# Inverse roots of a hybrid layer: the logarithm reads the sum of squares itself, and the correction takes three vector steps

## The chip, the cores and the metric

The kernel runs on one core of a Trainium2 chip. The metric is the device time in microseconds of one execution: the median of the runs shown. A core has engines that run side by side, each its own instructions in order: TensorE for matrix products (PE in the profile, its weight loads PEld), VectorE (DVE), ScalarE (ACT), GpSimd (POOL) and SyncE (SP), which here only issues transfers. Matrix products write to PSUM, a small memory of banks; everything else stands in SBUF. Instructions wait for each other through semaphores.

## What is computed

One layer over 576 frames: 512 of a new stream (the prompt) and 64 of a running one (the sample), 2048 channels each. All of it is float32.

```python
def rmsnorm(x, g):
    y = xf * lax.rsqrt(jnp.mean(xf * xf, axis=-1, keepdims=True) + EPS) * g

hn = rmsnorm(x, g_norm1)
q, k, v, gb, gc, hc = split(hn @ w_in)
q = rmsnorm(q.reshape(B, T, N_HEADS, HEAD_DIM), g_q)      # 8 heads of 128
k = rmsnorm(k.reshape(B, T, N_HEADS, HEAD_DIM), g_k)
o_attn = stick_breaking_blocks(q, k_all, v_all, P)
u = gc * hc
o_conv = gb * conv3(u)
mix = concat([rmsnorm(o_attn, g_attn_out), rmsnorm(o_conv, g_conv_out)])
x = x + mix @ w_out
h2 = rmsnorm(x, g_norm2)
x = x + (silu(h2 @ w_gate) * (h2 @ w_up)) @ w_down
```

There are six norms, each with an inverse root 1/sqrt(sum/n + EPS), EPS = 1e-6. The one of `g_norm1` is made with a power on GpSimd and is not touched. The other five go through the function that the change edits.

## The kernel before

**Layout.** Channels lie on the 128 partitions and frames along the free dimension, in two halves of 288 frames (`HALF`, `HALVES`). Nearly every vector or scalar instruction on activations is therefore 128x288. Each float32 operand of a product is split into a high and a low part (`split`, L221: a ScalarE copy rounds to the high part, a VectorE subtraction leaves the low part), and a product takes three matrix products (high by high, low by high, high by low; `step`, L210). Weights come by transfer and are split in the same way, 1024 columns at a time (`weight_parts`, L174, and later L1005 and L1008, L222 and L223).

**Stages.** Heads: for each of eight heads the products for q, k and v (`head`, `project`, `product`), and between them, in small pieces, the attention of the head before. Then the convolution channels (`conv_group`, `conv_run`), the output projection (`out_proj`), the gate and up products and the down products of the feed-forward part (`run`). The products after the second convolution group run by a scheme with seven products in place of eight, whose operands are sums and differences of blocks; `head_forms` makes those of the attention's output.

**Order.** TensorE's order is written out by hand. An object `pipe` counts products: after each three, `pipe.tick` lets generators that are due issue their next piece; `yield 13` means thirteen ticks later. VectorE's and ScalarE's orders are chosen by the framework's scheduler from the dependencies when the kernel is built, except in a few stretches under `manual_schedule`, where the program's order holds: the start up to L441, the stretch from the second convolution group (L934) to L1181, and the end from L1782.

**The inverse root.** `rsqrt_mean(dst, src, n, width)` (L456) gets in `src` the sum of squares over the channels, already on all partitions. `channel_sums` (L468) makes it with two matrix products by a matrix of ones, into a PSUM bank of the pair `misc`. The function then runs

- L461, VectorE: `ms = src / n + EPS`, out of PSUM into SBUF;
- L462 and L463, ScalarE: `y = exp(-0.5 ln(ms))`, a first value of the inverse root;
- L464, L465, L466, VectorE: one Newton correction, `dst = (1.5 - 0.5 ms y y) y`.

It is called from five places, for two halves each: `norm_evac` for q and for k of each head (L628; 32 calls), `head_forms` for the attention's output (L537; 2), `group_scale` for the convolution's output (L576; 2), `row_scale2` for the second norm (L1775; 2). In `norm_evac` the result `r` scales q or k (L629), which is then split for the attention scores (L679).

**The pair of banks `misc`.** `misc` (L260) hands out two PSUM banks in turn. A tile of it can be written only when the readers of the tile two before it are done. Its users in the heads are the sums (`ss`), the sample's scores (`zs`, L705), the weighted values (`po`, L744; `os`, L777) and the sample's cumulated logarithms (`cz`, L763). In a head past the first two the order on TensorE is: sums of q (two halves), `po`, sums of k first half, `cz`, sums of k second half, `os`, `zs`. So the tile two after the sums of k first half is that of the sums of k second half. In the first head the four sums stand in a row, two ticks or so apart (`lags`).

Of the kernel before, what the change touches and what calls it, by code (L numbers as in the profile page):

```python
# [10 lines left out]
F32 = mybir.dt.float32  # L11
F32R = mybir.dt.float32r
AF = mybir.ActivationFunctionType
ALU = mybir.AluOpType
PSUM = bass.MemoryType.PSUM

P = 128
# [3 lines left out]
HALF = T // 2  # L21
# [10 lines left out]
EPS = 1e-6  # L32
# [62 lines left out]
def tile_hybrid_stream_step(  # L95
# [6 lines left out]
    nc = tc.nc  # L102
# [13 lines left out]
    rpool = ctx.enter_context(tc.tile_pool(name="rpool", bufs=1, side="left"))  # L116
    tmp = ctx.enter_context(tc.tile_pool(name="tmp", bufs=2, side="left"))
# [44 lines left out]
    def weight_raw(i):  # L162
        src, nk, ncol = specs[i]
        raw = raw_tile["A"][:, i % 2, : nk * ncol]
        return raw, raw.rearrange("p (k c) -> p k c", k=nk), src
# [55 lines left out]
    def split(hi, lo, src, lo_eng=None):  # L221
        nc.scalar.copy(out=hi, in_=src)  # L222
        (lo_eng or nc.vector).tensor_tensor(out=lo, in0=src, in1=hi.bitcast(F32), op=ALU.subtract)  # L223
# [149 lines left out]
    with tc.manual_schedule(engines={mybir.EngineType.Activation, mybir.EngineType.DVE, mybir.EngineType.SP}):  # L373
        raw, raw3, src = weight_raw(0)
# [25 lines left out]
        for kt in range(KD + LAG):  # L400
# [21 lines left out]
            if kt == 16:  # L422
                nc.vector.tensor_tensor(out=lo1[:, :1024], in0=raws[1][:, :1024], in1=hi1[:, :1024].bitcast(F32),  # L423
                                        op=ALU.subtract)
# [28 lines left out]

    hpool.release()

    def rsqrt_mean(dst, src, n, width, ms=None, t=None):  # L456
        if ms is None:
            ms = tmp.tile([P, HALF], F32, tag="ms", name="ms", bufs=1)[:, :width]
            t = tmp.tile([P, HALF], F32, tag="t", name="t", bufs=1)[:, :width]
        y = tmp.tile([P, HALF], F32, tag="y", name="y")[:, :width]  # L460
        nc.vector.tensor_scalar(out=ms, in0=src, scalar1=1.0 / n, scalar2=EPS, op0=ALU.mult, op1=ALU.add)  # L461
        nc.scalar.activation(out=y, in_=ms, func=AF.Ln)  # L462
        nc.scalar.activation(out=y, in_=y, func=AF.Exp, scale=-0.5)  # L463
        nc.vector.tensor_tensor(out=t, in0=y, in1=y, op=ALU.mult)  # L464
        nc.vector.scalar_tensor_tensor(out=t, in0=t, scalar=-0.5, in1=ms, op0=ALU.mult, op1=ALU.mult)  # L465
        nc.vector.scalar_tensor_tensor(out=dst, in0=t, scalar=1.5, in1=y, op0=ALU.add, op1=ALU.mult)  # L466

    def channel_sums(src_hi, src_lo, a, b, name):  # L468
        ps = misc(name)[:, : b - a]
        mm(ps, oner, src_hi, start=True, stop=False)  # L470
        mm(ps, oner, src_lo, start=False, stop=True)
        return ps
# [10 lines left out]
    for i in range(5):  # L483
        n = P if i < 4 else TS
        nc.vector.tensor_scalar(out=dg[:n, i, :n], in0=ident[:n, :n], scalar1=rst[:n, i : i + 1], scalar2=None,
                                op0=ALU.mult)
# [40 lines left out]
    def head_forms():  # L527
# [8 lines left out]
        for (sh, sl), (a, b) in zip(two, HALVES):  # L536
            rsqrt_mean(acc_a[:, a:b], channel_sums(sh, sl, a, b, "ssg"), 8 * P, HALF)  # L537
            yield 4
# [28 lines left out]
    def group_scale(acc, dst, rows_of):  # L567

        four = cpool.tile([P, 2, 2, HALF], F32R, tag="uc", name="sqg")
        for i, (a, b) in enumerate(HALVES):  # L570
            sh, sl = four[:, i, 0], four[:, i, 1]
            split(sh, sl, acc[:, a:b])
            yield rows_of
            ss = channel_sums(sh, sl, a, b, "ssg")
            ms, t = (tmp.tile([P, HALF], F32, tag=tag, name=tag + "g") for tag in ("r", "sq"))
            rsqrt_mean(dst[:, a:b], ss, 8 * P, HALF, ms, t)  # L576
            yield rows_of

    acc_a = rpool.tile([P, T], F32, tag="R", name="acc_a", bufs=2)
# [39 lines left out]
    def norm_evac(name, gcol, dst_f, dst_hi, dst_lo, first, after=None):  # L619
        E = t1.tile([P, T], F32, tag="E", name=f"E{name}", bufs=2)  # L620

        def rest(a, b, sh, sl):
            if first:
                lags[0] += 4
            yield 6 + lags[0] if first else 16 if after else 13
            ss = channel_sums(sh, sl, a, b, "ss")
            r = tmp.tile([P, HALF], F32, tag="r", name="r")
            rsqrt_mean(r, ss, P, HALF)  # L628
            nc.vector.scalar_tensor_tensor(out=dst_f[:, a:b], in0=E[:, a:b], scalar=gcol, in1=r,  # L629
                                           op0=ALU.mult, op1=ALU.mult)  # L630
            e = min(b, TP)
            split(dst_hi[:, a:e], dst_lo[:, a:e], dst_f[:, a:e])
            if after and b == T:
                pipe.spawn(after)

        def evac(ps, a, b):
            nc.vector.tensor_tensor(out=E[:, a:b], in0=ps, in1=R1[:, a:b], op=ALU.mult)
            sq = tmp.tile([P, HALF], F32, tag="sq", name="sq")
            sh, sl = parts("sq")
            nc.scalar.activation(out=sq, in_=E[:, a:b], func=AF.Square)  # L640
            split(sh, sl, sq)
            pipe.spawn(rest(a, b, sh, sl))

        return evac
# [467 lines left out]
    def open_out():  # L1112

        xpool.release()
        bt["y"] = ypool = tc.alloc_tile_pool(name="ypool", bufs=1, reuse_waits="tile", side="right")
        x2t.extend(ypool.tile([P, 2, T], F32, tag=f"y{j}", name=f"x2_{j}") for j in range(NP))
        bt["m"] = tc.alloc_tile_pool(name="mpool", bufs=1, reuse_waits="tile", side="right")
        bt["mc"] = [bt["m"].tile([P, n, 2, HALF], F32R, tag=tag, name=f"mix{tag}")
                    for n, tag in ((NG, "m0"), (NG - 1, "m1"), (1, "m1z"))]
        bt["R"] = rpool.tile([P, T], F32, tag="R", name="R_c", bufs=2)  # L1120
        pipe.spawn(load_rest())
        pipe.spawn(state_out())
        pipe.spawn(group_scale(bt["acc"], bt["R"], 7), 7 * 28)
# [53 lines left out]
    for k_, (n, p_) in enumerate(corder):  # L1177
# [7 lines left out]
        if n == NCU - 1 and p_ in (6, 7, 4):  # L1185
            q = {6: 1, 7: 2, 4: 3}[p_]
            t = bt["pool"].tile([P, NH, 2, HALF], F32R, tag=f"t{q}", name=f"forms{q}")
# [430 lines left out]
    for d, v in visits.items():  # L1618
        n = next(a for a, b in zip(v, v[1:]) if a >= NGU + 10 and b >= a + 4)
# [228 lines left out]
```

## Time and profile before

| | |
|---|---|
| median of 3 runs | 2372.15 us (2371.21 to 2373.49) |
| the profiled execution, its own time | 2373.26 us |
| its span, first to last instruction | 2371.6 us |
| mean granted TensorE clock | 0.999 |
| TensorE busy | 2348.9 us, 99% of the span |
| VectorE, ScalarE, GpSimd busy | 81%, 49%, 12% |

Rows of groups of instructions give line, engine, operation, output and inputs, shape, count, and times. Rows of a time line give start and duration in microseconds and then the same; a bracket at the end says how long the engine stood idle before the instruction and what it waited for. Rows of waits give who waited for whom, the total in microseconds, the number of waits and the longest.

### The profile page before, as it was taken

How to read it: one execution, taken by the hardware profiler on the slowest of the kernel's cores; microseconds unless marked ns; L12 is line 12 of the kernel's file. 1: busy time of each engine (PE TensorE's matmuls, PEld its weight loads, DVE VectorE, ACT ScalarE, POOL GpSimd, SP SyncE). 2: the span in 40 equal slices, each digit the busy share in tenths (PEclk: the TensorE clock that was granted, in tenths of full speed). 3: DMA queues.
4: the chain of work that ended last, by engine and by line, in shares of the span. 5: the costliest groups of instructions: out<-in, count | busy, mean ns of one | idle time of the engine just before them, and what ended most of it. 6: DMA issues, size and time to landing. Idle time of an engine off the chain costs nothing.

```text
span 2371.6 us, 44043 instructions
## 1 busy us (share of the span) xinstructions
PE 2348.9 (99%) x17653; PEld 2338.0 (99%) x17653; DVE 1927.6 (81%) x2892; ACT 1166.2 (49%) x2083; POOL 290.5 (12%) x386
## 2 busy tenths in 40 slices
PE   8999999999999999999999999999999999999999
PEld 8999999999999999999999999999999999999999
DVE  7868776788887889888888888888888778887876
ACT  6656655444444555444444444444444444444444
POOL 2111111332111230000000000000000002431211
PEclk9999999999999999999999999999999999999999
DMA  8465554683368654444444444444444936886642
GB/s 259 127 179 165 138 148 111 219 263 118 109 235 220 195 166 147 140 152 135 138 152 136 138 152 137 137 152 137 137 152 132 359 112 213 224 225 199 205 131 82
DMA packets 563845, 395.75 MB, mean 167 GB/s; under 512 B 67006, under 2 KB 552760, under 8 KB 563640
## 3 DMA queue, kind: packets, MB, share of 16 engines
q1 hardware_dynamic: 554296, 376.39, 50.6%
q0 software_dynamic: 8624, 16.22, 3.4%
q8 instruction: 138, 2.26, 0.4%
q14 instruction: 67, 0.55, 0.1%
q10 hardware_dynamic: 720, 0.33, 0.0%
HBM read 301.45 MB, written 91.44 MB: 166 GB/s over the span
## 4 chain that ended last, share of the span: by engine, by line
PE 90%; DVE 5%; DMA 2%; ACT 2%; issue 1%; POOL 0%; ACTq 0%; SPq 0%; DVEq 0%; POOLq 0%
PE psy L1532 34%; PE psw L1532 17%; PE pj L213 12%; PE psx L1532 8%; PE psy L1036 6%; PE pjo L213 4%; PE psw L1036 3%; PE psx L1036 2%; DMA raw_a<-in_w_down_dram 1%; DVE whl L223 1%; PE po L747 1%; PE z L679 1%; DVE whl L1008 0%; PE os L777 0%; DMA raw_a<-in_w_in_dram 0%
## 5 line engine op out<-in xcount | busy, mean ns | idle before, releaser
L1532 PE MATMUL psy<-h_s,whl 128*128 128x288 f32 x2787 | 413.5, 295 | 0.3 <-ACT part L1542 0.3
L213 PE MATMUL pj<-x,whi 128*128 128x288 f32 x1856 | 389.9, 297 | 0.3 <-DVE x L356 0.2
L1532 PEld LDWEIGHTS psy<-h_s,whl 128*128 128x128 f32 x2787 | 384.8, 189 | 0.6 <-ACT part L1542 0.5
L223 DVE TENSOR_TENSOR whl<-raw_a,whl 128x1024 fp32r<-128x1024 f32 (+4 forms) x296 | 321.1, 1086 | 61.3 <-ACT whl L222 60.4
L1532 PE MATMUL psw<-t,whl 128*128 128x288 f32 x2400 | 348.3, 295 | 0.0
L1532 PEld LDWEIGHTS psw<-t,whl 128*128 128x128 f32 x2400 | 327.5, 188 | 0.0
L222 ACT CAST whl<-raw_a 128x1024 fp32r<-128x1024 f32 (+4 forms) x296 | 267.8, 906 | 115.2 <-issue 35.4
L213 PEld LDWEIGHTS pj<-x,whi 128*128 128x128 f32 x1856 | 304.1, 189 | 1.5 <-DVE x L356 1.0
L213 PE MATMUL pj<-x,wlo 128*128 128x288 f32 x928 | 274.1, 295 | 0.1
L223 DVE TENSOR_TENSOR whl<-raw_b,whl 128x1024 fp32r<-128x1024 f32 (+5 forms) x190 | 201.6, 1061 | 69.2 <-ACT whl L222 68.1
L222 ACT CAST whl<-raw_b 128x1024 fp32r<-128x1024 f32 (+5 forms) x190 | 165.1, 871 | 167.8 <-issue 73.4
L1542 ACT COPY part<-psy 128x288 f32<-128x288 f32 x242 | 96.6, 399 | 281.4 <-PE psy L1532 279.6
L1532 PE MATMUL psy<-b22m,whl 128*128 128x288 f32 x1212 | 183.3, 295 | 0.2 <-ACT part L1542 0.2
L1532 PE MATMUL psy<-t2t,whl 128*128 128x288 f32 x1212 | 182.9, 294 | 0.0
L213 PEld LDWEIGHTS pj<-x,wlo 128*128 128x128 f32 x928 | 174.5, 188 | 0.7 <-DVE wlo L423 0.3
L1532 PE MATMUL psx<-h_s,whl 128*128 128x288 f32 x1185 | 173.6, 294 | 0.0
L1532 PEld LDWEIGHTS psy<-b22m,whl 128*128 128x128 f32 x1212 | 168.2, 188 | 0.4 <-ACT part L1542 0.4
L1532 PEld LDWEIGHTS psy<-t2t,whl 128*128 128x128 f32 x1212 | 167.9, 188 | 0.0
L1532 PEld LDWEIGHTS psx<-h_s,whl 128*128 128x128 f32 x1185 | 162.3, 188 | 0.0
L222 ACT CAST whl<-s 128x1024 fp32r<-128x1024 f32 (+5 forms) x81 | 72.2, 892 | 102.2 <-PE psw L1532 100.9
L1311 POOL DMA_DIRECT2D hid_dram<-form x3 | 2.3, 751 | 947.6 <-DVE form L223 947.6
L1532 PE MATMUL psy<-t,whl 128*128 128x288 f32 x576 | 107.7, 297 | 0.0
(471 smaller groups left out, 4408.7 us busy)
## 6 DMA issues: line engine op xcount, KB each, us to landing
hid_dram<-form SPq DMA_DIRECT2D x147, 288.0 KB, 2.3
raw_a<-in_w_in_dram SPq DMA_DIRECT2D x41, 1024.0 KB, 5.8
raw_a<-in_w_gate_dram SPq DMA_DIRECT2D x22, 1024.0 KB, 6.0
raw_a<-in_w_up_dram SPq DMA_DIRECT2D x22, 1024.0 KB, 5.7
raw_b<-in_w_gate_dram SPq DMA_DIRECT2D x22, 1024.0 KB, 6.7
raw_b<-in_w_up_dram SPq DMA_DIRECT2D x22, 1024.0 KB, 7.0
h_s<-hid_dram SPq DMA_DIRECT2D x10, 2016.0 KB, 12.5
raw_a<-in_w_out_dram SPq DMA_DIRECT2D x16, 1024.0 KB, 5.6
```

Of the source, the lines that this page charges most:

```text
L213: mm(ps, w_[:, k, csl], x_, start=(k == 0 and n == 0), stop=(k == nk - 1 and n == 2))
L222: nc.scalar.copy(out=hi, in_=src)
L223: (lo_eng or nc.vector).tensor_tensor(out=lo, in0=src, in1=hi.bitcast(F32), op=ALU.subtract)
L679: mm(zb[i], a_[:, kk], b_[:, q0:TP], start=(n == 0), stop=False, skip_group_check=True)
L747: mm(po[:, i * P : 512], a_[:, i, :], b_[:, : 512 - i * P], stop=(i == 0 and n == 2), **kw)
L1036: mm(ps, whl[:, w_, j, :], x_, start=(start and j == 0 and q == 0), stop=(j == m - 1 and q == 2), skip_group_check=True)
L1311: q.dma_start(out=hid_dram[fp][2 * n - 2 : 2 * n].rearrange("f p t -> p f t"), in_=t.bitcast(F32))
L1532: mm(ps, whl[:, w_, j, :], x_, start=(start and j == 0 and q == 0), stop=(j == len(xs_) - 1 and q == 2), skip_group_check=True)
L1542: nc.scalar.copy(out=t, in_=st["y"])
```

## The change

`rsqrt_mean` loses its first step and the tile `ms`. ScalarE's logarithm reads the sums out of PSUM, with the division by n as its scale and EPS as its bias; the bias stands in a new column `epsc`, set once. The correction is rearranged: `t = -0.5/n y y`, then `t = (src + n EPS) t`, then `dst = (t + 1.5) y`. The second of these steps reads the sums out of PSUM too. `group_scale` passes one scratch tile fewer.

```diff
+    epsc = rpool.tile([P, 1], F32, name="epsc")
+    nc.vector.memset(epsc, EPS)
+
-    def rsqrt_mean(dst, src, n, width, ms=None, t=None):
-        if ms is None:
-            ms = tmp.tile([P, HALF], F32, tag="ms", name="ms", bufs=1)[:, :width]
+    def rsqrt_mean(dst, src, n, width, t=None):
+        if t is None:
             t = tmp.tile([P, HALF], F32, tag="t", name="t", bufs=1)[:, :width]
         y = tmp.tile([P, HALF], F32, tag="y", name="y")[:, :width]
-        nc.vector.tensor_scalar(out=ms, in0=src, scalar1=1.0 / n, scalar2=EPS, op0=ALU.mult, op1=ALU.add)
-        nc.scalar.activation(out=y, in_=ms, func=AF.Ln)
+        nc.scalar.activation(out=y, in_=src, func=AF.Ln, scale=1.0 / n, bias=epsc)
         nc.scalar.activation(out=y, in_=y, func=AF.Exp, scale=-0.5)
-        nc.vector.tensor_tensor(out=t, in0=y, in1=y, op=ALU.mult)
-        nc.vector.scalar_tensor_tensor(out=t, in0=t, scalar=-0.5, in1=ms, op0=ALU.mult, op1=ALU.mult)
+        nc.vector.scalar_tensor_tensor(out=t, in0=y, scalar=-0.5 / n, in1=y, op0=ALU.mult, op1=ALU.mult)
+        nc.vector.scalar_tensor_tensor(out=t, in0=src, scalar=n * EPS, in1=t, op0=ALU.add, op1=ALU.mult)
         nc.vector.scalar_tensor_tensor(out=dst, in0=t, scalar=1.5, in1=y, op0=ALU.add, op1=ALU.mult)
...
-            ms, t = (tmp.tile([P, HALF], F32, tag=tag, name=tag + "g") for tag in ("r", "sq"))
-            rsqrt_mean(dst[:, a:b], ss, 8 * P, HALF, ms, t)
+            t = tmp.tile([P, HALF], F32, tag="sq", name="sqg")
+            rsqrt_mean(dst[:, a:b], ss, 8 * P, HALF, t)
```

## The prediction

> **What bounds the kernel now.** I read the page first, its engines and its chain of work.
>
> ```profile
> span 2371.6 us, 44043 instructions
> PE 2348.9 (99%) x17653; PEld 2338.0 (99%) x17653; DVE 1927.6 (81%) x2892; ACT 1166.2 (49%) x2083; POOL 290.5 (12%) x386
> ...
> PE 90%; DVE 5%; DMA 2%; ACT 2%; issue 1%; POOL 0%; ACTq 0%; SPq 0%; DVEq 0%; POOLq 0%
> ```
>
> TensorE is busy all but 22.7 us of the span. The change touches no matrix product, so it can only win out of waits of TensorE, or make new ones. The next view is therefore that of TensorE's waits, in the stretch of the heads (50 to 440 us) and in the one behind it (440 to 530 us); the last row is from 770 to 910 us.
>
> ```profile
> PE z L679 <- ACT kh L222: 2.0, 1, 2.0
> PE ss L470 <- DVE ms L461: 0.9, 1, 0.9
> PE po L747 <- DVE vl L223: 0.6, 1, 0.6
> PE ss L470 <- ACT sq L222: 0.4, 1, 0.4
> PE z L679 <- DVE kl L223: 0.3, 1, 0.3
> ...
> PE psy L1036 <- DVE whl L1008: 1.8, 2, 1.0
> PE psx L1036 <- DVE cv L1060: 1.5, 1, 1.5
> PE psw L1036 <- DVE whl L1008: 0.5, 1, 0.5
> ...
> PE ss L470 <- ACT sq L222: 1.6, 1, 1.6
> ```
>
> These are 4.2 us in the heads and 3.8 us behind them, 8.0 us in all: the most that less work on VectorE can give back near the 34 calls that lie there. The four later calls (from 774 us and from 890 us) have no TensorE wait behind them in that view; the last row's 1.6 us there is a wait of the sums for their own operand, ahead of the function. I put them at 0.
>
> **The steps and their durations.** The lines of the function, whole run:
>
> ```profile
> L461 DVE TENSOR_SCALAR ms<-ss x34: 444/453/458, 50.7 to 898.9; 128x288 f32<-128x288 f32 x34
> L462 ACT ACTIVATE y<-ms x36: 434/444/448, 51.5 to 900.1; 128x288 f32<-128x288 f32 x36
> L464 DVE TENSOR_TENSOR t<-y x36: 445/452/2575, 52.5 to 901.4; 128x288 f32<-128x288 f32 x36
> L465 DVE SCALAR_TENSOR_TENSOR t<-t,ms x36: 442/456/461, 55.1 to 902.1; 128x288 f32<-128x288 f32 x36
> ```
>
> Removed: 38 vector steps of 0.453 us, 17.2 us of VectorE's busy time. In VectorE's queue each is worth less, since instructions overlap by their ends: the first `ms` of the time line below starts at 56.22 us and its follower at 56.58, so 0.36 to 0.37 us apiece.
>
> The step that goes from a product of two tensors to one with a factor keeps its price: L464 and L465 stand at 452 and 456 ns, and L465 already has the form that L464 takes. The step that now reads PSUM in place of SBUF: L461 reads PSUM in 453 ns, L465 reads SBUF in 456, so 0. The logarithm with another source, a scale and a bias column isn't in this trace. Its bounds are a plain copy out of PSUM and an activation with a column from SBUF:
>
> ```profile
> L1045 ACT COPY part<-psy x50: 379/400/403, 494.5 to 777.8; 128x288 f32<-128x288 f32 x50
> L598 ACT ACTIVATE o_ob<-o_ob,g1c x8: 522/535/537, 76.4 to 336.3; 128x288 f32<-128x288 f32 x8
> L287 DVE MEMSET nhalf<- x1: 62/62/62, 1.7 to 1.7; 128x5 f32 x1
> ```
>
> That is -0.04 to +0.09 us beside 0.444; I take 0, since ScalarE is idle half the time and its neighbours hide either. Over the four calls of one head the worst end is 0.36 us of ScalarE, over all 38 it is 3.4 us, and uncovered only where ScalarE is the last to come. The new memset costs 0.06 us of VectorE once, by L287, under the weight splits of the same time; uncovered it is 0.06 us.
>
> What the change moves is the release of a PSUM bank. Before, the bank of a sum was free when L461 had read it; now it is free only when the second correction step has, behind two activations and two vector steps. What is queued behind a late bank is TensorE itself, in its written order.
>
> **Head 0.** Here the four sums stand closest. Rows of four engines' time lines, in order of time:
>
> ```profile
> 49.77 4.99 POOL L176 TENSOR_TENSOR wlo<-raw_a,whi 128x1024 fp32r<-128x1024 f32 x2 [10.02 <-ACT whi L175]
> 52.49 2.58 DVE L464 TENSOR_TENSOR t<-y 128x288 f32<-128x288 f32 x1
> 53.95 0.29 PE L470 MATMUL ss<-sq,oner 128*128 128x288 f32 x1
> 55.10 0.46 DVE L465 SCALAR_TENSOR_TENSOR t<-t,ms 128x288 f32<-128x288 f32 x1
> 56.22 0.45 DVE L461 TENSOR_SCALAR ms<-ss 128x288 f32<-128x288 f32 x1
> 56.58 0.51 DVE L629 SCALAR_TENSOR_TENSOR qf<-Eq,gqs,r 128x288 f32<-128x288 f32 x1
> 56.70 0.44 ACT L462 ACTIVATE y<-ms 128x288 f32<-128x288 f32 x1 [3.72 <-DVE ms L461]
> 56.81 0.37 PE L470 MATMUL ss<-sq,oner 128*128 128x288 f32 x1 [0.85 <-DVE ms L461]
> 68.90 0.38 PE L679 MATMUL z<-qh,kh 128*128 128x256 f32 x1 [2.04 <-ACT kh L222]
> ```
>
> VectorE's first square of y takes 2.58 us, up to 55.07, while GpSimd works until 54.76; the same line takes 0.45 elsewhere. I take it that the step in its place is held just as long, since it also reads y twice from SBUF. The second step then ends at 55.10 + 0.46 = 55.56. The third sum, which takes the bank of the first, started at 53.95 without a wait; now it starts at 55.56 at the earliest: a new wait of 1.61 us. The old wait of 0.85 us at the fourth sum goes away: TensorE comes there at 56.81 - 0.85 + 1.61 = 57.57. The bank of the second sum must be free by then. Its logarithm no longer stands behind a vector step (ScalarE idled 3.72 us for that), and VectorE needs a split, the third step and two new steps after 55.56, some 4 x 0.37 = 1.5 us, so 57.1. That holds by 0.5 us.
>
> TensorE so reaches the scores 0.76 us later than before, where it waited 2.04 us; 1.28 us of wait are left. From 55 us to the scores VectorE's queue is nearly without a gap, and it has three `ms` steps fewer (those of the second, third and fourth sum): 3 x 0.37 = 1.1 us. The scores start 1.1 us earlier, and of the 1.28 us some 0.2 are left as a wait. **Head 0: -1.1 us.** If VectorE's saving doesn't arrive there, it is 0 (the new wait is hidden under the old); if the scores come late by the whole new wait, +0.76.
>
> Behind this the Trainium skill has a rule, on the page "SBUF — State Buffer", section "SBUF: two separate sides": VectorE and GpSimd share a pair of ports under an exclusive lock, which a vector instruction with two SBUF inputs needs and one that holds it keeps for its whole length. The 2.58 us beside GpSimd's 4.99 us agree. By that rule the new first step is held as the old was, as taken above; if the new form escaped it, that step would end at 52.95, the third sum would not wait, and the 2.9 us of waits in this head could go whole: -2.9 us in place of -1.1.
>
> **The heads behind it.** Closest is the first half of k, whose bank is wanted again by the second half. The tightest case is in head 3, a usual one in head 4.
>
> ```profile
> 195.10 0.29 PE L471 MATMUL ss<-sq,oner 128*128 128x288 f32 x1
> 197.34 2.40 DVE L176 TENSOR_TENSOR wlo<-raw_a,whi 128x1024 fp32r<-128x1024 f32 x2
> 201.41 0.45 DVE L465 SCALAR_TENSOR_TENSOR t<-t,ms 128x288 f32<-128x288 f32 x1
> 202.17 0.29 PE L470 MATMUL ss<-sq,oner 128*128 128x288 f32 x1
> ...
> 242.89 0.29 PE L471 MATMUL ss<-sq,oner 128*128 128x288 f32 x1
> 247.83 0.44 DVE L465 SCALAR_TENSOR_TENSOR t<-t,ms 128x288 f32<-128x288 f32 x1
> 249.96 0.29 PE L470 MATMUL ss<-sq,oner 128*128 128x288 f32 x1
> ```
>
> L465 stands where the new releasing step stands. It ends at 201.86, 0.31 us ahead of the next sum, and at 248.27, 1.69 us ahead. The step removed came before it in the chain, so it should come no later than now: no new wait. TensorE has almost no wait in these heads to win either (0.6 for `vl`, 0.4 for `sq`, both near the start). **Heads 1 to 7: 0**, with -1.0 (those two gone) at one end; the other end is the first rival below.
>
> **The attention's output, 444 us on.** The chain of waits leaves TensorE at 444 us and runs over VectorE and GpSimd to the waits of 490 to 530 us.
>
> ```profile
> 447.59 0.38 DVE ms L461
> ```
>
> Both `ms` steps lie in VectorE's queue here, and this one on the chain. Two fewer are 2 x 0.37 = 0.74 us, which can come out of the 3.8 us of waits there. **-0.7 us**, with 0 (GpSimd's differences, which the chain also runs over, take it back) and -1.5 (the logarithms start at once, before the queue) as ends.
>
> **Sum.** -1.1 + 0 - 0.7 = -1.8 us, against the profiled execution's own 2373.26 us (span 2371.6 and 1.7 around it): 2371.5. That execution lies 1.1 us above the median of the runs; from the median it is 2372.15 - 1.8 = **2370.3 us**.
>
> **Rivals.**
>
> *The bank is held too long* (slower). Place: the sums of k, second half, in heads 2 to 7, and the third sum of head 0. The order on VectorE is chosen anew when the kernel is built. If the releasing step falls behind one more weight split (two halves, 2.40 us less the overlap of 0.12, 2.28), it ends after the next sum is due. Taking the usual slack of 1.69 for four heads and the tight 0.31 for two, TensorE waits 4 x 0.59 + 2 x 1.97 = 6.3 us, and head 0 adds its 0.76: 7.1 us, 2379.2. It decides from a delay of 0.31 us in the tight heads and 1.69 in the others. For it: the slack in head 3 is small, and a wait there has no later wait to hide in. Against: the chain to the release gets shorter by a step, and that split already lies ahead of it at 197.34.
>
> *Hidden anyway.* ScalarE, not VectorE, is the last to come: the logarithm now waits for its place among ScalarE's casts, as the `ms` step waited before. Then neither head 0 nor the stretch from 444 us wins, and the new wait hides under the 2.04 us: 2372.2. For it: 17.2 us of busy time are saved on an engine that TensorE waits for in only 8.0 us. Against: VectorE's queue is full in just the two stretches with waits.
>
> *All waits go.* VectorE gets far enough ahead that the 8.0 us in both stretches vanish: 2364.2. Against: 3.8 us of them hang on weight splits and GpSimd as well.
>
> *The form escapes the hold at 52.49* (the rule above not applying): -2.9 + 0 - 0.7, 2368.6.
>
> **How the numbers follow.** What a measurement of this kernel can tell from no change is about 0.2%, 4.7 us: 2367.4 to 2376.9. Forecast 0.45; hidden anyway 0.27; the form escapes 0.06; all waits go 0.10; the bank held too long 0.12. The first three lie within 0.2% (0.78, and 0.02 of the all-waits case that stops short of it): same 0.80. Faster takes 0.08 of the all-waits case, slower 0.12. The range reaches from 4.3 us under the forecast (two thirds of the way to the case in which all waits go) to 4.3 over the old time (more than half of the held bank's 7.1): 2366.0 to 2376.5; the first leaves some 0.07 below, the other about 0.11 above.
>
> **What would show it.** Right: TensorE waits at the third sum of head 0 for the second correction step, some 1.6 us, and no longer for L461 at the fourth; its wait at the first scores shrinks to a few tenths and they start near 67.8 us; VectorE's busy time falls by some 17 us; no new waits on `ss` past 100 us. Wrong: waits of TensorE on `ss` in heads 2 to 7, for the step that reads PSUM; the first scores later than 69 us; waits between 490 and 530 us that stay at 3.8 us or grow; a first square at 52 us that takes 0.45 us.

## The result, and the profile after

| | median, us | range | runs |
|---|---|---|---|
| before | 2373.2 | 2371.21 to 2375.35 | 6 |
| changed | 2381.8 | 2378.67 to 2385.37 | 6 |

The ratio is 1.0037, with a 95% interval of 1.0026 to 1.0047: the changed kernel is slower by 8.6 us at the medians, and lies outside the predicted range. The profiled execution of the changed kernel took 2378.67 us, the fastest of its six. Its trace is 5.4 us longer than that of before (2377.0 against 2371.6), so it shows some two thirds of the loss; the rest is spread between executions.

From the page of the changed kernel, its span and engines:

```profile
span 2377.0 us, 44012 instructions
PE 2353.5 (99%) x17653; PEld 2343.8 (99%) x17653; DVE 1907.0 (80%) x2855; ACT 1168.0 (49%) x2083; POOL 288.0 (12%) x386
```

VectorE has 20.6 us less to do, as it should. TensorE has the same 17653 products as before, and is *busy* for 4.6 us more (2353.5 against 2348.9). That is the first sign that the loss isn't a wait: 23.5 us of the span are without a product, 22.7 before.

TensorE's waits in the changed kernel, 50 to 440 us, and behind the dots 440 to 530 us:

```profile
PE ss L471 <- DVE t L466: 2.9, 2, 2.2
PE po L748 <- DVE vl L223: 0.7, 1, 0.7
PE ss L471 <- ACT sq L222: 0.4, 1, 0.4
PE ss L472 <- DVE sq L223: 0.2, 1, 0.2
...
PE psy L1037 <- DVE whl L1009: 2.4, 3, 1.0
PE psx L1037 <- DVE cv L1061: 1.5, 1, 1.5
PE psw L1037 <- DVE whl L1009: 0.5, 1, 0.5
PE psy L1037 <- ACT whl L1006: 0.3, 1, 0.3
```

4.2 us in the heads, as before, and 4.7 behind them (3.8 before). In the heads the composition is new: the two waits for the step that now releases the bank, 2.9 us, stand for the waits at the scores and at L461, which are gone. Both are in head 0. Its time line in the changed kernel, TensorE, VectorE and one row of GpSimd:

```profile
50.66 4.96 POOL L176 TENSOR_TENSOR wlo<-raw_a,whi 128x1024 fp32r<-128x1024 f32 x2 [10.46 <-ACT whi L175]
50.73 0.29 PE L471 MATMUL ss<-sq,oner 128*128 128x288 f32 x1
53.43 2.50 DVE L465 SCALAR_TENSOR_TENSOR t<-y 128x288 f32<-128x288 f32 x1
55.86 0.45 DVE L223 TENSOR_TENSOR sq<-sq 128x288 fp32r<-128x288 f32 x1
56.23 0.45 DVE L466 SCALAR_TENSOR_TENSOR t<-ss,t 128x288 f32<-128x288 f32 x1
56.82 0.37 PE L471 MATMUL ss<-sq,oner 128*128 128x288 f32 x1 [2.20 <-DVE t L466]
58.01 0.70 DVE L804 STREAM_TRANSPOSE kcT<-cK 128x512 f32<-128x512 f32 x1
58.97 0.45 DVE L466 SCALAR_TENSOR_TENSOR t<-ss,t 128x288 f32<-128x288 f32 x1
59.56 0.37 PE L471 MATMUL ss<-sq,oner 128*128 128x288 f32 x1 [0.66 <-DVE t L466]
69.43 0.28 PE L680 MATMUL z<-qh,kh 128*128 128x256 f32 x1
...
69.92 0.42 PE L680 MATMUL z<-qh,kh 128*128 128x384 f32 x1
```

The third sum waits for the releasing step, and the scores start with no wait at all. So this stretch doesn't lose time either. To see where it is lost, I took the start of the same product in both traces. The difference, changed less before, is the time lost or won up to there:

| at, us | +50 | 72 | 480 | 690 | 910 | 1850 | 1900 | end |
|---|---|---|---|---|---|---|---|---|
| changed less before, us | +0.5 | -0.1 | -0.6 | +1.3 | -0.7 | +3.8 | +4.9 | +5.4 |

Up to 910 us the two traces come out even: 1.9 us are lost between 480 and 690 us and come back by 910, in part because the profiled execution of before had a granted clock of only 0.72 from 894 to 900 us. Nearly the whole loss arises between 910 and 1850 us, the gate and up products of the feed-forward part, where none of the edited code runs. The view of windows over this stretch, first the kernel before, then the changed one (time of the window, then busy time and number of instructions of PE, PEld, DVE, ACT, POOL, then granted clock, DMA share, GB/s):

```profile
530.00:690.00 160.00, 160.00 (x1212) 160.00 (x1212) 139.38 (x188) 70.15 (x97) 29.64 (x43) 1.00 0.43 133
910.00:1850.00 940.00, 940.00 (x7112) 940.00 (x7111) 791.40 (x1081) 438.56 (x657) 1.78 (x2) 1.00 0.46 144
```

```profile
530.00:690.00 160.00, 160.00 (x1208) 160.00 (x1207) 138.77 (x186) 69.90 (x97) 28.89 (x41) 1.00 0.43 130
910.00:1850.00 940.00, 940.00 (x7077) 940.00 (x7076) 788.42 (x1077) 436.55 (x655) 0.83 (x1) 1.00 0.45 142
```

TensorE is busy for every microsecond of both windows, at the full granted clock, and gets 35 products fewer done: 940/7112 = 132.17 ns for a product in the one, 940/7077 = 132.82 in the other. 35 products are 4.6 us. The products themselves have become slower, and not all of them. The groups by line and shape in 910 to 1850 us, before and then changed (busy time, then mean ns of one):

```profile
L1532 PE MATMUL psw<-t,whl 128*128 128x288 f32 x2017 | 280.4, 294 | 0.0
L1532 PE MATMUL psy<-h_s,whl 128*128 128x288 f32 x1764 | 240.4, 294 | 0.0
L1532 PE MATMUL psy<-b22m,whl 128*128 128x288 f32 x903 | 126.6, 295 | 0.0
L1532 PE MATMUL psy<-t2t,whl 128*128 128x288 f32 x903 | 126.4, 294 | 0.0
```

```profile
L1533 PE MATMUL psw<-t,whl 128*128 128x288 f32 x2016 | 280.2, 294 | 0.0
L1533 PE MATMUL psy<-h_s,whl 128*128 128x288 f32 x1764 | 242.1, 296 | 0.0
L1533 PE MATMUL psy<-b22m,whl 128*128 128x288 f32 x899 | 125.9, 294 | 0.0
L1533 PE MATMUL psy<-t2t,whl 128*128 128x288 f32 x882 | 124.5, 296 | 0.0
```

Products over `t` and `b22m` are as before; those over `h_s` and `t2t` are longer. The mean time from the start of such a product to the start of the next over the same tile went from 132.3 to 133.3 ns for `h_s` (the `psy` group) and from 132.2 to 133.3 for `t2t`, while `t` stayed (132.2 and 132.1). What tells the two kinds apart is where the tile lies. `epsc` is a column of 4 bytes, and the program as it is built gives it 32 bytes of each partition, at the end of `rpool`. Every pool that is put on the left-hand stack after that starts 32 bytes later, among them that of `h_s` and `t2t` (`h_s` at byte 72480 instead of 72448 of each partition); `t` and `b22m` lie elsewhere and didn't move.

### The profile page after: what moved, and what is told of

Read it like the earlier page. It is cut to its first block, busy times and chain, and to the rows that moved or that the text cites. A ratio compares the mean times of both kernels' runs of the same rounds, so it can differ in the third digit from the quotient of the medians.

```text
span 2377.0 us, 44012 instructions
## 1 busy us (share of the span) xinstructions
PE 2353.5 (99%) x17653; PEld 2343.8 (99%) x17653; DVE 1907.0 (80%) x2855; ACT 1168.0 (49%) x2083; POOL 288.0 (12%) x386
## 4 chain that ended last, share of the span: by engine, by line
PE 91%; DMA 4%; DVE 2%; ACT 2%; issue 1%; POOL 0%; SPq 0%; ACTq 0%; DVEq 0%; POOLq 0%
PE psy L1533 35%; PE psw L1533 17%; PE pj L213 12%; PE psx L1533 9%; PE psy L1037 6%; PE pjo L213 4%; PE psw L1037 3%; PE psx L1037 1%; DMA raw_a<-in_w_in_dram 1%; DMA forms<-form_dram 1%; DMA xs_t<-xs_dram 1%; DMA form_dram<-hf 1%; PE po L748 1%; PE z L680 0%; DMA xin<-in_x_prompt_dram 0%
```

## The experiments

Two theories were set against each other first: the loss comes from the place that `epsc` takes; or it comes from the new arithmetic (the bank held longer, ScalarE's longer logarithm). No kernel leaves out any of the computation. Kernels measured together share their runs of the kernel before.

**The changed kernel once more**, unedited, beside the others (before: 2372.64 us, 24 runs).

> The changed kernel as it is, as the mark for the runs beside it. Both theories: 1.0026 to 1.0047 of the kernel before, 5 to 11 us over it; matrix products on tiles of the left pools (h_s, t2t, xs_t) start 0.133 to 0.134 us apart, those on the right pools (t, b22m, x) 0.132.

2380.71 us (2379.3 to 2382.06), ratio 1.0029, interval 1.0017 to 1.0042. The loss comes again.

**The arithmetic without the place.** EPS goes into a sixth column of `nhalf`, whose five columns of 4 bytes already take 32 bytes, so no pool moves. (Without `ms`, some scratch tiles inside `tmp` change places, by 1152 or 2304 bytes, here as in the changed kernel.) The edit of the changed kernel:

```diff
-    nhalf = const.tile([P, 5], F32, name="nhalf")
+    nhalf = const.tile([P, 6], F32, name="nhalf")
+    nc.vector.memset(nhalf[:, 5:6], EPS)
...
-    epsc = rpool.tile([P, 1], F32, name="epsc")
-    nc.vector.memset(epsc, EPS)
+    epsc = nhalf[:, 5:6]
```

> The change with its five instructions as they are, but EPS stands in a sixth column of nhalf, inside bytes that were padding, so no tile moves. Theory place (the new column moves every later tile of the left side by 32 bytes, and matrix products that read a moved tile start about 1 ns later each): within 2 us of the kernel before, ratio 0.999 to 1.0008, and 0.132 us apart on h_s and t2t. Theory bank (the bank of the sums is held longer and TensorE waits): as the changed kernel, 1.0026 to 1.0047, with the same waits on ss.

2370.99 us (2369.48 to 2373.9), ratio 0.9993, interval 0.9984 to 1.0001. The loss is gone with the place. Three views of this kernel: its window, its waits in the heads, and its time line there.

```profile
910.00:1850.00 940.00, 940.00 (x7111) 940.00 (x7110) 790.60 (x1079) 438.32 (x657) 0.77 (x1) 1.00 0.46 144
```

```profile
PE ss L471 <- DVE t L466: 2.0, 2, 1.4
```

```profile
50.79 0.29 PE L471 MATMUL ss<-sq,oner 128*128 128x288 f32 x1
56.09 0.38 PE L471 MATMUL ss<-sq,oner 128*128 128x288 f32 x1 [1.43 <-DVE t L466]
...
69.18 0.42 PE L680 MATMUL z<-qh,kh 128*128 128x384 f32 x1
```

7111 products, as before the change, and head 0 still has the new waits. The medians are 1.65 us apart, but the interval holds no change: the arithmetic alone is not shown to win, and it doesn't lose.

**The place without the arithmetic.** The kernel before with two lines more, and nothing reads the column:

```diff
+    epsc = rpool.tile([P, 1], F32, name="epsc")
+    nc.vector.memset(epsc, EPS)
```

> The kernel before with the new column and its memset, and nothing else: four correction steps as before. Theory place: slow, ratio 1.002 to 1.005, with 0.133 to 0.134 us on h_s, t2t and xs_t. Theory bank: 1.000.

2380.14 us (2377.9 to 2382.49), ratio 1.0029, interval 1.0018 to 1.004: 7.5 us for a column that nobody reads. Its window:

```profile
910.00:1850.00 940.00, 940.00 (x7077) 940.00 (x7077) 789.86 (x1078) 436.45 (x656) 0.93 (x1) 1.00 0.45 142
```

**The change, with the place given back.** `lpad`, a pool of 32 bytes that lies between `tmp` and the later pools and holds no data, is left out of the changed kernel. `tmp` still lies 32 bytes later, all pools behind it are back at their old places:

```diff
-    lpad = ctx.enter_context(tc.tile_pool(name="lpad", bufs=1, side="left"))
-    lpad.tile([P, 8], F32, name="lpad_t")
```

> The changed kernel without the 32-byte pad behind the pool tmp: tiles of tmp stay moved by 32 bytes, all behind it stand where they stood before. Theory place, if the tiles of the big pools matter: as the kernel before, 0.999 to 1.0008. If it is the tiles of tmp: as the changed kernel. Theory bank: as the changed kernel, 1.0026 to 1.0047.

2372.69 us (2368.73 to 2375.7), ratio 0.9998, interval 0.9989 to 1.0007. The loss is gone, so `tmp` isn't what matters, but the pools behind it are.

```profile
910.00:1850.00 940.00, 940.00 (x7111) 940.00 (x7110) 790.65 (x1080) 438.48 (x658) 1.58 (x2) 1.00 0.46 144
```

The four runs settle the first question: the place. A different order of instructions is no rival: as built, the kernel with the column alone has on every engine the same instructions in the same order as the kernel before, with one memset more, and the kernels below that only move tiles have exactly those of the kernel before. The next ones, each on the kernel before, ask which tiles and which distances (before beside them: 2373.7 us, 23 runs).

**64 bytes instead of 32**, for the pools behind `tmp`. The theory was that a tile should start on a multiple of 64 bytes, as its pool did before:

```diff
-    lpad.tile([P, 8], F32, name="lpad_t")
+    lpad.tile([P, 24], F32, name="lpad_t")
```

> The kernel before with 64 bytes more in the pad behind tmp, so that all the tiles that moved by 32 bytes move by 64. Theory place in steps of 64 bytes (an operand of 1152 bytes touches one more 64-byte piece when it starts in the middle of one): as before, 0.999 to 1.0008, products on h_s and t2t 132.1 to 132.4 ns apart. Theory place in steps of 128 or 256 bytes: slow again, 1.001 to 1.004, 133 ns.

2384.88 us (2382.08 to 2386.09), ratio 1.0044, interval 1.0032 to 1.0056: no better than the column alone (1.0029, with an interval that overlaps), and the theory of 64 bytes falls.

```profile
910.00:1850.00 940.00, 940.00 (x7074) 940.00 (x7073) 789.91 (x1077) 436.52 (x656) 0.91 (x1) 1.00 0.46 142
```

**The feed-forward tiles alone, by 32 bytes**, with an empty pool ahead of theirs; heads and convolution stay where they were:

```diff
+    h2pad = tc.alloc_tile_pool(name="h2pad", bufs=1, side="left")
+    h2pad.tile([P, 8], F32, name="h2pad_t")
...
+    h2pad.release()
```

> The kernel before with a 32-byte pad ahead of the pool of the feed-forward operands alone (h_s, h_z, t2t, ta move; heads and convolution stay). Theory place by the moved operand: 35 products fewer between 910 and 1850 us, some 5 us over the kernel before, ratio 1.0015 to 1.003, and up to 890 us no loss. If the heads' and the convolution's tiles carry the loss: 1.000 to 1.001.

2380.07 us (2376.73 to 2383.13), ratio 1.0025, interval 1.0017 to 1.0034. Most of the loss is made by these tiles alone.

```profile
530.00:690.00 160.00, 160.00 (x1212) 160.00 (x1211) 139.63 (x187) 70.06 (x97) 29.31 (x41) 1.00 0.43 132
910.00:1850.00 940.00, 940.00 (x7076) 939.92 (x7075) 788.91 (x1077) 437.07 (x654) 1.50 (x2) 1.00 0.46 142
```

The convolution's window (530 to 690 us) is back at 1212 products, the feed-forward's stays at 7076. Each stage pays for its own tiles.

**The weights' tiles by 32 bytes**, everything else as before. `lpad` goes, and its 32 bytes stand in `const`, ahead of the weights' pool; `rpool` and `tmp` move too:

```diff
-    lpad = ctx.enter_context(tc.tile_pool(name="lpad", bufs=1, side="left"))
-    lpad.tile([P, 8], F32, name="lpad_t")
...
+    const.tile([P, 8], F32, name="const_pad")
```

> The kernel before with the 32-byte pad ahead of the weights in place of behind tmp: the split weights (the operand that is loaded and stands still) and the raw weights move by 32 bytes, the frames' operands stand where they stood. Theory place, for the operand that streams alone: 0.999 to 1.0008. If any operand counts, every one of 17653 products gets about 1 ns: 18 us, 1.007.

2389.28 us (2378.17 to 2392.68), ratio 1.005, interval 1.003 to 1.007. Its six times fall in two groups, two at 2378.17 and 2379.13 us and four from 2388.58 on, which I can't explain. The window and two groups of products there (`t` had 294 ns and `b22m` 295 before):

```profile
910.00:1850.00 940.00, 940.00 (x7052) 940.00 (x7052) 790.15 (x1081) 437.09 (x655) 1.47 (x1) 1.00 0.46 141
```

```profile
L1531 PE MATMUL psw<-t,whl 128*128 128x288 f32 x2030 | 284.7, 297 | 0.0
L1531 PE MATMUL psy<-b22m,whl 128*128 128x288 f32 x882 | 124.5, 297 | 0.0
```

60 products fewer, and the products over `t` and `b22m`, which didn't move, are longer now (those over `h_s` and `t2t` stand at 297 too). The theory that only the place of the streamed operand counts falls: the place of the weights counts too, or that of something else that moved with them.

**The feed-forward tiles by 64, 128 and 256 bytes**: the same pad as above with 16, 32 and 64 columns (before beside them: 2371.99 us, 19 runs).

> As feed_forward_moved, with 64 bytes in place of 32. Theory A (64-byte pieces of the moved operand): no loss, 7112 products from 910 to 1850 us. Theory B (a longer period, or the operands' places to each other): a loss as in moved_64_bytes, 7074 to 7080 products, and the products on t and b22m, which do not move, slow down as well (132.8 and 133.6 ns in place of 132.2 and 132.4).

> As feed_forward_moved, with 128 bytes. Theory A: no loss, 7112. Theory B with a period of 128: no loss; with a period of 256: a loss, under 7100 products from 910 to 1850 us.

> As feed_forward_moved, with 256 bytes. Theory A and a period of 128 or 256: no loss, 7112. A period of 512 or more, or a loss that comes from any move at all: under 7100.

| moved by | median, us | range | ratio | products, 910 to 1850 us |
|---|---|---|---|---|
| 32 bytes (above) | 2380.07 | 2376.73 to 2383.13 | 1.0025 (1.0017 to 1.0034) | 7076 |
| 64 | 2381.19 | 2378.98 to 2382.04 | 1.0041 (1.0026 to 1.0056) | 7073 |
| 128 | 2374.45 | 2371.55 to 2376.49 | 1.001 (1.0001 to 1.002) | 7110 |
| 256 | 2372.79 | 2369.58 to 2374.49 | 1.0003 (0.9994 to 1.0013) | 7112 |

The windows of 64, 128 and 256 bytes, in this order; for the last two the down products from 2030 us on as well:

```profile
910.00:1850.00 940.00, 940.00 (x7073) 939.97 (x7072) 788.92 (x1077) 435.61 (x653) 1.47 (x1) 1.00 0.46 142
```

```profile
910.00:1850.00 940.00, 940.00 (x7110) 939.82 (x7109) 792.45 (x1082) 437.69 (x657) 2.37 (x2) 1.00 0.46 144
2030.00:2350.00 320.00, 319.86 (x2419) 319.57 (x2418) 257.19 (x344) 142.77 (x263) 84.80 (x95) 1.00 0.61 180
```

```profile
910.00:1850.00 940.00, 940.00 (x7112) 940.00 (x7111) 792.16 (x1082) 437.54 (x657) 1.77 (x2) 1.00 0.46 144
2030.00:2350.00 320.00, 319.74 (x2424) 319.46 (x2423) 256.69 (x344) 143.53 (x266) 85.64 (x95) 1.00 0.60 180
```

Of these four distances, 256 bytes cost nothing that can be told and 128 nearly nothing (2 products here, 5 in the down products), 32 and 64 the full price. The kernel before has 2424 down products in the last window too. With 64 bytes the products over `t` and `b22m`, which didn't move, are longer as well (by their starts from 132.2 to 132.8 and from 132.5 to 133.7 ns):

```profile
L1534 PE MATMUL psw<-t,whl 128*128 128x288 f32 x2016 | 281.2, 295 | 0.0
L1534 PE MATMUL psy<-b22m,whl 128*128 128x288 f32 x887 | 125.5, 296 | 0.0
```

A look at the addresses as built adds something. In the kernel before, the tiles of these products all start at multiples of 256 bytes (`whl` at 19200, 27392, 35584 and 43776, `h_s` at 72448, `t2t` at 130048, `b22m` at 173824). Moves by 128 and 256 bytes keep multiples of 128; those by 32 and 64 bytes, of frames or of weights, don't. That fits a step of 128 bytes for both operands, but it doesn't explain the slower products on tiles that stayed, and no run here tests it further.

**A version that beats both.** With the place out of the way, what is left of the change is head 0 with its new waits. The kernel with EPS in the spare bytes, and the third and fourth sum of head 0 five ticks later, so that products stand between the second sum and the third:

```diff
-                lags[0] += 4
+                lags[0] += 9 if lags[0] == 8 else 4
```

> The change with EPS in spare bytes, and in the first head the third and fourth sum issued five ticks (2 us) later. Theory: the waits on ss for the second correction step at 54 and 58 us, 2.0 us in all, go, and what VectorE does not hold back at the first scores is won: 0 to 2 us under eps_in_spare_bytes, ratio to the kernel before 0.9985 to 0.9995. If the first scores then wait for VectorE as they did before the change: no gain, 0.9993.

2369.65 us (2367.54 to 2372.17) against 2373.7, ratio 0.9983, interval 0.9974 to 0.9991: faster than the kernel before, by 4.05 us at the medians. Two rows of its time line, the third and the fourth sum:

```profile
56.20 0.38 PE L471 MATMUL ss<-sq,oner 128*128 128x288 f32 x1
58.95 0.37 PE L471 MATMUL ss<-sq,oner 128*128 128x288 f32 x1 [0.62 <-DVE t L466]
```

The third sum no longer waits. The interval overlaps that of the kernel without the later sums (0.9984 to 1.0001), so how much of the 4 us the five ticks bring is not shown. In one trace each, the same stretch of products, from 50 to 480 us, takes 3.5 us less than before here and 1.7 us less without the later sums.

## Why the prediction was wrong

**The step that failed** is "The new memset costs 0.06 us of VectorE once": the column was costed as an instruction, and the place it takes was not costed at all. In the runs the column by itself costs 7.5 us (2380.14 against 2372.64), over four times the forecast gain. The premise behind it, "The change touches no matrix product, so it can only win out of waits of TensorE, or make new ones", holds for the code and fails for the addresses: the products themselves became slower. No rival reached this. "The bank is held too long" gave a time close to the result (2379.2) from a wrong cause: in the changed trace no sum past 100 us waits for the releasing step, and the kernel with the same held banks and the old places has lost nothing. Two of the prediction's signs of being wrong did come (scores later than 69 us; longer waits behind 440 us), but neither marks the loss: at 690 us the changed trace is only 1.3 us behind, and at 910 us 0.7 us ahead.

**The sum without the column** came near: -1.8 us forecast, -1.65 at the medians of the kernel with EPS in spare bytes. Its interval, about -3.8 to +0.2 us, holds no change, so this total isn't shown, and one of its two terms did not arrive.

- *Head 0, -1.1 us.* From the first sum to the first of the 384-wide score products, which is behind the last of the scores' waits, it takes 70.06 - 50.24 = 19.8 us before, 69.92 - 50.73 = 19.2 in the changed trace and 69.18 - 50.79 = 18.4 with EPS in spare bytes: -0.6 and -1.4, around the forecast. One trace against one would not show this, but other runs bear it out: in the four traces of the `feed_forward` kernels, whose heads are those of before, the stretch takes 19.6 to 19.9 us, and in the other trace with the new arithmetic and the old places (`lpad` left out) 18.7. The new wait at the third sum came (forecast 1.61; 2.20 and 1.43) and the wait at the scores went. The fourth sum was to be free "by 0.5 us" and waits 0.66 and 0.62: between the two releasing steps VectorE also runs the scaling L630 and the transpose L804 (0.44 and 0.62 us until the next step starts), which I hadn't counted, and the others take 0.34 to 0.49 us each, so the second release comes 2.74 us after the first, not 1.5. The scores start at 69.43, not near 67.8; 0.5 us of this is that the whole stretch came late, by its first sum. The two rows of the kernel before:

```profile
50.24 0.29 PE L470 MATMUL ss<-sq,oner 128*128 128x288 f32 x1
...
70.06 0.42 PE L679 MATMUL z<-qh,kh 128*128 128x384 f32 x1
```

- *The hold of the first square.* It takes 2.50 us in the changed kernel beside GpSimd's split (50.66 to 55.62 us), and 2.58 before. The form with a factor is held as the plain product was, as the rule of the Trainium skill (page "SBUF — State Buffer", section "SBUF: two separate sides") has it; the rival by which it escapes falls.
- *Heads 1 to 7, 0.* No new wait there. In the seven heads the bank of k's first half comes free between 1.4 and 5.5 us ahead of its next sum.
- *The stretch from 444 us, -0.7 us.* It did not arrive. The waits there are 4.7 us in the changed trace and 4.1 with EPS in spare bytes, 3.8 before; the waits for weight splits (`whl`) and for the convolution (`cv`) are no shorter than they were, so the two vector steps fewer didn't reach them. From 480 to 530 us the changed trace loses 1.3 us to that of before, the one with EPS in spare bytes 0.2.
- *VectorE's busy time, -17 us.* -20.6; the 3.4 beyond the removed step I haven't assigned. *The logarithm*: 0.495 us in the rows below, 0.05 over the old form and inside the bounds of -0.04 to +0.09.

From the changed kernel's groups by line, whole run (shortest/median/longest ns):

```profile
L463 ACT ACTIVATE y<-ss,epsc x34: 482/495/504, 52.4 to 894.1; 128x288 f32<-128x288 f32 x34
L466 DVE SCALAR_TENSOR_TENSOR t<-ss,t x34: 440/450/461, 56.2 to 901.2; 128x288 f32<-128x288 f32 x34
```

The step that reads PSUM in place of SBUF (L466) costs 0.450 us against 0.456, so nothing, as put.

## What to carry to other kernels

Cost a new tile by its bytes as well as by its instructions: ask which tiles lie behind it on its stack and how far they move, and put small constants into bytes that an existing tile already occupies, or shrink a pad by as much. Here a move by 256 bytes cost nothing that can be told, and one by 32 or 64 the full price. When a loss shows up far from the edited code with TensorE busy throughout, compare the count of products in one fixed window and the mean of one by operand: waits will show nothing. A new tile can slow a kernel whose layout happened to suit it; the cheapest test is the kernel before with the tile alone.

## What the runs showed of the hardware

The rate of 128x288 products depends on where operands lie in SBUF. With TensorE busy throughout and a granted clock of 1.00 over 940 us, moving tiles by 32 bytes took the start-to-start time of a product on a moved tile from 132.2 or 132.3 ns to between 133.1 and 133.4. Moving them by 64 slowed some of these (`t2t` to 133.4 or 133.5, `h_s` into `psy` to 133.0) and not others (`h_s` into `psx`, 132.3), and slowed products on tiles that stayed (`b22m` from 132.5 to 133.7). Both cost 35 to 39 of 7112 products in 940 us; 128 bytes cost 2 of them, 256 none. Why is open. That the place of the streamed operand alone decides is refuted: moving weights, `rpool` and `tmp` by 32 bytes took 60 products, over all operands. Nor is it known why the kernel with moved weights falls into two groups of times some 10 us apart.
